# The output projection of a decoder layer: its weight sums made in DRAM, its weight blocks streamed

## The chip, the cores and the metric

The kernel runs on one core of a Trainium2 chip. The metric is the device time of one execution in microseconds (us); lower is better. The time before is the median of three executions.

## The reference

One decoder layer, in float32, for one sequence of 512 tokens and a model width of 2048: adaLN conditioning, one input projection, then two branches (sliding-window attention with sinks, and a gated DeltaNet), a gated merge, and an output projection that is added to the input:

```python
mod = jax.nn.silu(c) @ w_ada + b_ada
shift, scale, gate = jnp.split(mod[:, None, :], 3, axis=-1)
h = rms_norm(x, norm_w) * (1.0 + scale) + shift
proj = h @ w_in
aq, ak, av, ag, d_qkv, dz, db, da, mg_a, mg_b = jnp.split(proj, _split_points(), axis=-1)
...
a_out = swa_attention(aq, ak, av, sinks).astype(x.dtype) * jax.nn.silu(ag)
y_a = a_out @ w_o_swa
...
g = -jnp.exp(a_log.astype(f32)) * jax.nn.softplus(da.astype(f32) + dt_bias.astype(f32))
o = gated_delta_rule(dq, dk, dv, g, beta)
o = rms_norm(o, dn_norm_w) * jax.nn.silu(dz.reshape(B, T, DN_V_HEADS, DN_HEAD_V).astype(f32))
y_b = o.reshape(B, T, DN_VAL).astype(x.dtype) @ w_o_dn

y = jax.nn.sigmoid(mg_a) * y_a + jax.nn.sigmoid(mg_b) * y_b
return x + gate * (y @ w_out)
```

The change concerns the last product, `y @ w_out` (512 × 2048 by 2048 × 2048), and where its weights are prepared.

## The kernel before, in words

**Products.** Every float32 product is made of three products of a reduced type (`mm3`, L237): each operand is split into a high part (`whi`, a cast on ScalarE, L52) and a low part (`wlo`, a subtraction on VectorE, L53), and TensorE makes high × high, high × low and low × high. Weights come in 1 MiB blocks of 128 × 2048 into a pool `wraw` of two buffers (`load_job`, L195, the DMA of L200), and are split by halves of 128 × 1024 into a pool `whl` of three buffers each of `whi` and `wlo`. `channel_tile` (L244) makes one 128-channel output of 48 matmuls from two halves, and calls `pump` after every two triples. `pump` is what interleaves the work: it loads and splits the next weights (`weight_tick`), and takes a step of other generators: `live` ones with delays, `slow` ones with a budget, and `side` ones, which `beside(gen, rate, queue)` registers and which advance by `rate` steps per call.

**Stages.** Startup with the adaLN sums; the keys and decay gates of the DeltaNet, with the triangular solves beside them; the heads of the DeltaNet (16 groups, `heads`); the projection of that branch; attention; and `finish`, which projects the attention's result (`os`, 16 tiles), merges both branches into y (kept in DRAM as `y_d`) and calls `output`.

**The keys' stage around the change.** SP (SyncE) issues almost all DMAs, in the order of its instruction stream. For each head pair the stage issues and computes: `E<-g_rows`, a broadcast row per head; the mask product and `affine_select` on POOL (GpSimd; `decay_mask`, L710); an exponential on ScalarE; a product with the keys' own product on VectorE.

**The output stage.** `output` uses a Strassen-Winograd scheme: seven products m1 to m7 in place of eight, over two column halves n, each product in four pieces: 56 items of 12 matmuls. Their left operands are parts of y: a11, a12 and s3, which the `os` loop keeps, and s1, s2, s4, a22, which the generator `combos` (L1301) makes one step per item from rows of `y_d` (tiles ya and yc; the first eight steps make s1 and s2, the next eight a22 and s4). The right operands are blocks of `w_out` or sums of them: four of the seven products (m7, m5, m6, m4) need a sum. Before the change, three slots a, b, c of two blocks each hold raw blocks (a in `wraw`, b and c in a pool `fraw`), and VectorE adds slots in place (`add`, L1345, the instruction of L1347) ahead of the split, in an order of products m1, m7, m5, m2, m6, m4, m3 that lets each sum be made from the last. Sixteen blocks are loaded. `prep(i)` splits the weights of an item two items ahead; `evict` and `columns` add the products, the gate and the input x and store.

Of the kernel before, what the change touches and what calls it, by code (L numbers as in the profile page):

```python
# [7 lines left out]
F32 = mybir.dt.float32  # L8
# [3 lines left out]
ALU = mybir.AluOpType  # L12
# [4 lines left out]
P = 128  # L17
# [19 lines left out]
class Layer:  # L37
# [552 lines left out]
    def deltanet(self):  # L590
        tc, nc, a = self.tc, self.nc, self.a
        dram = self.dram
        self.lt_d = dram.tile([2, 2, 16, 4, HD, HD], F32, name="lt_d")
        self.lab_d = dram.tile([VH, HD, 4, HD], F32, name="lab_d")
        self.ta_d = dram.tile([2, 16, 4, HD, HD], F32, name="ta_d")
        self.ts_d = dram.tile([2, 2, 16, 4, HD, HD], F32, name="ts_d")
        self.kT_d = dram.tile([KH, P, T], F32, name="kT_d")
        self.k_d = dram.tile([KH, P, T], F32, name="k_d")
        self.o_d = dram.tile([VH, P, T], F32, name="o_d")
        with ExitStack() as ps:  # L600
            self.pmm = ps.enter_context(tc.tile_pool(name="pmm", bufs=2, space=PSUM, reuse_waits="tile"))
            self.ptp = ps.enter_context(tc.tile_pool(name="ptp", bufs=2, space=PSUM, reuse_waits="tile"))
            self.gwk = ps.enter_context(tc.tile_pool(name="gwk", bufs=1, reuse_waits="tile"))
            sol1 = ps.enter_context(tc.tile_pool(name="sol1", bufs=1, side="right", reuse_waits="tile"))
            with ExitStack() as sa:
                wk = sa.enter_context(tc.tile_pool(name="dnA", bufs=2, reuse_waits="tile"))
                sol0 = sa.enter_context(tc.tile_pool(name="sol0", bufs=1, reuse_waits="tile"))
                gp = sa.enter_context(tc.tile_pool(name="gates", bufs=1, reuse_waits="tile"))
                self.go(self.gates(gp), 1)
                self.keys_done, self.solve_in = [], {}  # L610
                self.keep_order = True
                for g in range(NST):
                    self.go(self.keys(wk, g, self.acc_k[g]), 10 + 8 * g)
                for j in range(NFIRST):
                    self.merge_gate("mb", j, self.mb_d)
                self.go(self.solve_load(sol0, 0), 1)
                self.go(self.solve_load(sol1, 1), 1)
                s0 = self.paced(self.solve(sol0, 0, nc.vector), 0.82)
                s1 = self.paced(self.solve(sol1, 1, nc.vector), 0.0)
                for kind, j in self.mixed():  # L620
                    if kind == "k":
                        self.go(self.keys(wk, j, self.channel_tile(f"k{j}")), 0)
                    else:
                        self.merge_gate("mb", j, self.mb_d)
                        if j == KT - 3:
                            s0[1] = 1.2
                for j in range(3):
                    self.merge_gate("ma", j, self.ma_d)
                    if s0 not in self.slow:
                        s1[1] = 1.1  # L630
                self.drain_live()
                self.drain_slow(s0)
                self.keep_order = False
                s1[1] = 0.6
            with ExitStack() as sb:
                wk = sb.enter_context(tc.tile_pool(name="dnB", bufs=2, reuse_waits="tile"))
                self.tt = []
                for n in range(4):
                    t = wk.tile([P, NTB, P], F32, tag=f"tt{n}", name=f"tt{n}", bufs=1)
                    nc.gpsimd.memset(t[HD:P, :, 0:HD], 0.0)  # L640
                    self.tt.append(t)
                for g in range(KH):
                    if g == 8:
                        self.drain_slow(s1)
                    self.heads(wk, g)
                for j in range(3, 5):
                    self.merge_gate("ma", j, self.ma_d)
                self.drain_live()
        self.dump("o", self.o_d)

    def keys(self, wk, g, ps):

# [66 lines left out]
    def solve_load(self, wk, b):  # L719
# [16 lines left out]
        yield 4  # L736
        self.solve_in[b] = A, bet

# [532 lines left out]
    def finish(self):  # L1271
        tc, nc, a = self.tc, self.nc, self.a
        with ExitStack() as es:
            yp = es.enter_context(tc.tile_pool(name="fy", bufs=1, reuse_waits="tile"))
            wk = es.enter_context(tc.tile_pool(name="fwk", bufs=2, reuse_waits="tile"))
            quad = lambda pool, name: tuple(pool.tile([P, 8, 256], F32R, name=name + x) for x in "hl")
            A = {n: quad(yp, n) for n in ("a11", "s3", "a12")}
            lo, hi = slice(0, 256), slice(256, 512)
            with ExitStack() as eo:
                self.pmm = eo.enter_context(tc.tile_pool(name="pmmf", bufs=2, space=PSUM, reuse_waits="tile"))  # L1280
                for j in range(KT):
                    m = wk.tile([P, T], F32, tag="m", name="m")
# [18 lines left out]
    def combos(self, wk, A):  # L1301
# [4 lines left out]
        for second in range(2):  # L1306
            for kt in range(8):
# [15 lines left out]
                n = "s4" if second else "s2"  # L1323
                self.split(A[n][0][:, kt, :], A[n][1][:, kt, :], p[:, lo])

    def output(self, es, wk, A):

        tc, nc, a = self.tc, self.nc, self.a
        pf = es.enter_context(tc.tile_pool(name="pfo", bufs=1, space=PSUM, reuse_waits="tile"))
        fr = es.enter_context(tc.tile_pool(name="fraw", bufs=1, reuse_waits="tile"))  # L1330
        slots = {}

        def load(slot, c, r, nchunk):

            for i in range(2):
                if slot == "a":
                    t = self.wraw.tile([P, 2048], F32, tag="raw", name="raw")
                else:
                    t = fr.tile([P, 2048], F32, tag=f"{slot}{i}", name=f"raw{slot}")
                nc.sync.dma_start(out=t, in_=a["w_out"][2 * c + nchunk, 2 * r + i])  # L1340
                slots[slot, i] = t

        piece = lambda slot, p: slots[slot, p // 2][:, (p % 2) * 1024 : (p % 2) * 1024 + 1024]

        def add(x, y):  # L1345
            def f(p):
                nc.vector.tensor_tensor(out=piece(x, p), in0=piece(x, p), in1=piece(y, p), op=ALU.add)  # L1347

            return f

        order = [
            ("m1", "a11", "a", []),
            ("m7", "s3", "b", [add("a", "b"), add("b", "c")]),
            ("m5", "s1", "a", []),
            ("m2", "a12", "b", []),
            ("m6", "s2", "a", [add("a", "c")]),
            ("m4", "a22", "b", [add("b", "a")]),
            ("m3", "s4", "c", []),
        ]
        items = [(n, m, p) for n in range(2) for m in range(7) for p in range(4)]  # L1360
        ready = {}
        after = {
            ("m1", 3): [], ("m7", 3): [("b", 0, 1)],
            ("m4", 3): [("a", 0, 0), ("b", 1, 0)], ("m3", 3): [("c", 1, 1)],
        }

        def prep(i):
            if i >= len(items):
                return
            n, m, p = items[i]  # L1370
            name, _, slot, sums = order[m]
            for f in sums:
                f(p)
            hi = self.whl.tile([P, 1024], F32R, tag="whi", name="whi")
            lo = self.whl.tile([P, 1024], F32R, tag="wlo", name="wlo")
            self.split(hi, lo, piece(slot, p))
            ready[i] = (hi, lo)
            for s, c, r in after.get((name, p), []):
                if name == "m7":
                    load(s, c, r, n)  # L1380
                elif n == 0:
                    load(s, c, r, 1)

        side = self.combos(wk, A)
        next(side, None)
        load("a", 0, 0, 0)
        load("b", 1, 0, 0)
        load("c", 1, 1, 0)
        todo = []
        keep = {}  # L1390
        ps = {}
# [44 lines left out]
        for i in range(2):  # L1436
            prep(i)
        for i, (n, m, p) in enumerate(items):
            name, s, slot, _ = order[m]
            if p == 0:  # L1440
                for t in range(2):
                    m7 = name == "m7"
                    ps[name, t] = pf.tile([P, T], F32, tag=f"y{t}" if m7 else "r", name=name, bufs=1 if m7 else 6)
            hi, lo = ready.pop(i)
            ah, al = A[s]
            for kk in range(2):
                kt = 2 * p + kk
                w = slice(kk * T, kk * T + T)
                for t in range(2):
                    tsl = slice(t * P, (t + 1) * P)  # L1450
                    self.mm3(ps[name, t], (ah[:, kt, tsl], al[:, kt, tsl]), (hi[:, w], lo[:, w]), kt == 0, kt == 7)
                if kk == 0:
                    prep(i + 2)
                    for f in todo:
                        evict(*f)
                    todo = []
                    next(side, None)
            if p == 3:
                todo.append((n, name))
# [108 lines left out]
```

## Time and profile before

| | |
|---|---|
| runs | 2933.2, 2930.87, 2933.1 us (median 2933.1) |
| span of the profiled execution | 2929.7 us |
| TensorE (PE) busy | 2870.6 us, 98% of the span |
| VectorE (DVE) busy | 1787.2 us, 61% |
| ScalarE (ACT) busy | 1085.1 us, 37% |
| GpSimd (POOL) busy | 243.0 us, 8% |
| bytes moved by DMA | 451.11 MB, 154 GB/s on average |
| output stage (`output`) | about 2752 to 2922 us |

The table is from the profiled execution on the one core, whose span is the time from its first to its last instruction; the runs are timed apart from it. In the rows of the prediction, PE is a matmul, PEld the load of its stationary operand; `x48` counts instructions; "L53" is a line of the kernel before; "<-" names what an operation reads, or what ended a wait. A window's row has its stretch, its length, the busy time of PE, PEld, DVE, ACT and POOL with counts, the clock granted to TensorE (1.00 is full), the busy share of the DMA engines, and GB/s. A row of a group has busy time, the mean of one in ns, and idle time before.

### The profile page before, as it was taken

To read this page: it belongs to the slowest core of one execution; us is meant where nothing else is said; L and a number is where in the kernel's file an instruction comes from. 1 tells how busy PE (TensorE), PEld (TensorE's weight loads), DVE (VectorE), ACT (ScalarE), POOL (GpSimd) and SP (SyncE) were. 2 spreads that over 40 slices of the span, in tenths; PEclk is the share of its full clock that TensorE was granted. 3 is DMA by queue.
4 is the path that set the end of the run, shared out by engine and by line. 5 is a ranking of instruction groups with operands and counts; after the bars stand their busy time and mean duration, and the time that the engine had idled before them with its cause. 6 is when DMAs were issued, how large, how long until landed. Compare 5 with 4: busy or idle time off the path is not lost.

```text
span 2929.7 us, 38073 instructions
## 1 busy us (share of the span) xinstructions
PE 2870.6 (98%) x14556; PEld 2351.2 (80%) x14556; DVE 1787.2 (61%) x2915; ACT 1085.1 (37%) x2113; POOL 243.0 (8%) x204
## 2 busy tenths in 40 slices
PE   8899999999999999999999999999999999999988
PEld 6677888888888888888888788888787877888867
DVE  6775998777776545544444553434655655553697
ACT  4355333333334333333333322212343443432343
POOL 0022211100000110000000000000100000000022
PEclk9999999999999999999999999999999999999999
DMA  9747555633334533333332675554322223375562
GB/s 387 281 147 219 163 169 159 203 109 111 125 113 134 160 116 124 115 122 109 123 109 100 235 263 182 186 172 141 105 89 94 85 89 103 119 262 172 173 194 97
DMA packets 175046, 451.11 MB, mean 154 GB/s; under 512 B 72433, under 2 KB 74993, under 8 KB 138897
## 3 DMA queue, kind: packets, MB, share of 16 engines
q1 hardware_dynamic: 174866, 448.70, 46.1%
q8 instruction: 114, 1.87, 0.3%
q14 instruction: 66, 0.54, 0.1%
HBM read 386.95 MB, written 59.45 MB: 152 GB/s over the span
## 4 chain that ended last, share of the span: by engine, by line
PE 84%; DVE 3%; DMA 2%; issue 1%; ACT 1%; POOL 1%; SPq 0%; POOLq 0%; DVEq 0%; ACTq 0%
PE mm L240 24%; PE mm L242 24%; PE mm L241 24%; DVE wlo L53 1%; PE S L1208 1%; PE pv L918 1%; PE po L937 1%; PE O L1259 1%; PE pP L274 1%; PE po L936 1%; PE pd L933 1%; PE pp L908 1%; PE m L241 1%; PE m L242 1%; PE m L240 1%
## 5 line engine op out<-in xcount | busy, mean ns | idle before, releaser
L240 PE MATMUL mm<-hh,whi 128*128 128x512 f32 x2784 | 1130.7, 406 | 2.3 <-ACT whi L52 1.6
L242 PE MATMUL mm<-hh,wlo 128*128 128x512 f32 x2784 | 1089.6, 391 | 1.3 <-DVE wlo L53 1.3
L241 PE MATMUL mm<-hl,whi 128*128 128x512 f32 x2784 | 1087.3, 391 | 0.0
L53 DVE TENSOR_TENSOR wlo<-raw,whi 128x1024 fp32r<-128x1024 f32 (+1 forms) x452 | 554.4, 1229 | 491.5 <-ACT whi L52 481.7
L52 ACT CAST whi<-raw 128x1024 fp32r<-128x1024 f32 (+1 forms) x452 | 470.7, 1044 | 972.9 <-PE mm L241 927.3
L242 PEld LDWEIGHTS mm<-hh,wlo 128*128 128x128 f32 x2784 | 522.6, 188 | 115.1 <-DVE wlo L53 2.2
L240 PEld LDWEIGHTS mm<-hh,whi 128*128 128x128 f32 x2784 | 523.7, 188 | 112.3 <-issue 8.4
L241 PEld LDWEIGHTS mm<-hl,whi 128*128 128x128 f32 x2784 | 524.2, 188 | 98.7 <-issue 0.4
L240 PE MATMUL mm<-oh,whi 128*128 128x512 f32 x512 | 200.6, 393 | 2.6 <-ACT oh L52 1.7
L242 PE MATMUL mm<-oh,wlo 128*128 128x512 f32 x512 | 199.4, 390 | 0.5 <-DVE wlo L53 0.5
L241 PE MATMUL mm<-ol,whi 128*128 128x512 f32 x512 | 199.5, 390 | 0.1
L865 POOL TENSOR_TENSOR qe<-qe,yq 128x512 f32<-128x512 f32 x32 | 51.4, 1624 | 902.7 <-DMA qe<-eg_rows 836.9
L714 POOL TENSOR_TENSOR E<-E,neg_g 128x512 f32<-128x512 f32 x64 | 78.4, 1224 | 476.2 <-DMA E<-g_rows 342.8
L240 PEld LDWEIGHTS mm<-oh,whi 128*128 128x128 f32 x512 | 96.0, 188 | 24.8 <-ACT oh L52 3.0
L241 PEld LDWEIGHTS mm<-ol,whi 128*128 128x128 f32 x512 | 96.1, 188 | 22.2 <-DVE ol L53 1.3
L764 DVE TENSOR_TENSOR A<-A,atmp 128x62 f32<-128x62 f32 (+30 forms) x124 | 112.9, 911 | 1.5
L242 PEld LDWEIGHTS mm<-oh,wlo 128*128 128x128 f32 x512 | 96.1, 188 | 20.9 <-DVE wlo L53 1.3
L757 DVE TENSOR_TENSOR atmp<-A 128x62 f32<-128x62 f32 (+30 forms) x124 | 109.3, 882 | 1.5
L911 DVE SCALAR_TENSOR_TENSOR r<-pp,neg_eg,vt 128x128 f32<-128x128 f32 x96 | 29.2, 346 | 78.8 <-PE pp L908 77.6
L1232 ACT ACTIVATE sm<-sm,mx,rs 128x256 f32<-128x256 f32 (+1 forms) x128 | 71.7, 561 | 3.3 <-DVE mx L1227 3.3
L580 DVE SCALAR_TENSOR_TENSOR yv<-mm,convh,yv 128x511 f32<-128x511 f32 (+2 forms) x96 | 71.5, 745 | 1.6
L241 PE MATMUL m<-wlo,hh 128*128 128x512 f32 x128 | 51.8, 404 | 10.1 <-DVE wlo L53 10.1
(331 smaller groups left out, 3145.6 us busy)
## 6 DMA issues: line engine op xcount, KB each, us to landing
raw<-in_w_ch SPq DMA_DIRECT2D x158, 1024.0 KB
wa<-in_w_ada_ss SPq DMA_DIRECT2D x32, 1024.0 KB
raw<-in_w_od SPq DMA_DIRECT2D x32, 1024.0 KB
E<-g_rows SPq DMA_DIRECT2D x64, 256.0 KB
gw<-in_w_ada_gate SPq DMA_DIRECT2D x16, 1024.0 KB
raw<-in_w_os SPq DMA_DIRECT2D x16, 1024.0 KB
qe<-eg_rows SPq DMA_DIRECT2D x32, 256.0 KB
o_d<-zh SPq DMA_DIRECT2D x32, 256.0 KB
```

Of the source, the lines that this page charges most:

```text
L52: self.nc.scalar.copy(out=hi, in_=src)
L53: self.nc.vector.tensor_tensor(out=lo, in0=src, in1=hi.bitcast(F32), op=ALU.subtract)
L240: nc.tensor.matmul(ps, lhsT=wh, rhs=xh, start=first, stop=False)
L241: nc.tensor.matmul(ps, lhsT=wh, rhs=xl, start=False, stop=False)
L242: self.last_mm = nc.tensor.matmul(ps, lhsT=wl, rhs=xh, start=False, stop=last).ins
L274: self.nc.tensor.transpose(dst[:, c * P : (c + 1) * P], src_cols(c), self.ident)
L580: nc.vector.scalar_tensor_tensor(out=y[:, s:], in0=ps[:, : T - s], scalar=w[:, j : j + 1], in1=y[:, s:], op0=ALU.mult, op1=ALU.add)
L714: nc.gpsimd.tensor_tensor(out=E, in0=E, in1=ng, op=ALU.add)
L757: eng.tensor_tensor(out=t, in0=A[:, m : m + 1, m + 1 :].to_broadcast([P, m, n]), in1=A[:, :m, m : m + 1].to_broadcast([P, m, n]), op=ALU.mult,
L764: eng.tensor_tensor(out=A[:, :m, m + 1 :], in0=A[:, :m, m + 1 :], in1=t, op=ALU.add)
L865: nc.gpsimd.tensor_tensor(out=qf, in0=qf, in1=q, op=ALU.mult)
L1232: nc.scalar.activation(t, t, AF.Exp, scale=r[:, h : h + 1], bias=mx[:, h : h + 1], accum_out=den[:, h : h + 1])
```

## The change

The four sums for each of the four block positions (two column halves n, two row halves i) are made in DRAM, into sixteen new tensors `ws_d` of 1 MiB, by the DMA engines: a block or an earlier sum is copied within DRAM on SP, then a second block is added to it by an accumulating transfer that POOL issues. m7 and m5 are each a copy and an accumulate of blocks; m6 copies m7 and adds a block; m4 copies m6 and adds another. `weight_sums` is registered with `beside` at the start of the heads' stage, at a rate of 0.15 steps per call.

The output stage then loads 28 blocks, one for each two items, in the order of their use: blocks of `w_out` for m1, m2, m3 and the sums for the rest, into a pool of four buffers (`out_load`). The first four are loaded ahead of the `os` loop, each next one when a block's second piece has been split. The additions on VectorE are gone. The order of the products becomes m1, m2, m7, m5, m6, m4, m3: m2 moves ahead of m7 and m5.

```diff
+        self.ws_d = {k: dram.tile([P, 2048], F32, name=f"ws{k[0]}{k[1]}{k[2]}") for k in self.sum_keys()}
...
+                self.beside(self.weight_sums(), 0.15, "ws")
                 for g in range(KH):
...
                 self.drain_live()
+                self.drain("ws")
...
+    def weight_sums(self):
+        nc = self.nc
+        for n in range(2):
+            for i in range(2):
+                w = lambda c, r: self.a["w_out"][2 * c + n, 2 * r + i]
+                m7, m5, m6, m4 = (self.ws_d[s, n, i] for s in ("m7", "m5", "m6", "m4"))
+                steps = [
+                    [(m7, w(1, 0), w(1, 1)), (m5, w(0, 0), w(1, 0))],
+                    [(m6, m7, w(0, 0))],
+                    [(m4, m6, w(0, 1))],
+                ]
+                for parts in steps:
+                    for dst, src, _ in parts:
+                        nc.sync.dma_start(out=dst, in_=src)
+                    for _ in range(2):
+                        yield
+                    for dst, _, more in parts:
+                        nc.gpsimd.dma_start(out=dst, in_=more, accum_op=ALU.add, max_dma_last_dim=8192)
+                    for _ in range(2):
+                        yield
...
+            self.wpool = es.enter_context(tc.tile_pool(name="fraw", bufs=4, reuse_waits="tile"))
+            for _ in range(4):
+                self.out_load()
...
+    def out_order(self):
+        return [
+            ("m1", "a11", (0, 0)), ("m2", "a12", (0, 1)), ("m7", "s3", None), ("m5", "s1", None), ("m6", "s2", None),
+            ("m4", "a22", None), ("m3", "s4", (1, 1)),
+        ]
+
+    def out_load(self):
+        j = self.wnext
+        if j < 28:
+            n, m, i = j // 14, j // 2 % 7, j % 2
+            name, _, q = self.out_order()[m]
+            t = self.wpool.tile([P, 2048], F32, tag="raw", name="raww")
+            src = self.a["w_out"][2 * q[0] + n, 2 * q[1] + i] if q else self.ws_d[name, n, i]
+            self.nc.sync.dma_start(out=t, in_=src)
+            self.wtiles[j] = t
+            self.wnext += 1
...
-        def add(x, y):
-            def f(p):
-                nc.vector.tensor_tensor(out=piece(x, p), in0=piece(x, p), in1=piece(y, p), op=ALU.add)
...
-            name, _, slot, sums = order[m]
-            for f in sums:
-                f(p)
             hi = self.whl.tile([P, 1024], F32R, tag="whi", name="whi")
             lo = self.whl.tile([P, 1024], F32R, tag="wlo", name="wlo")
-            self.split(hi, lo, piece(slot, p))
+            self.split(hi, lo, self.wtiles[i // 2][:, (i % 2) * 1024 : (i % 2) * 1024 + 1024])
             ready[i] = (hi, lo)
-            for s, c, r in after.get((name, p), []):
-                if name == "m7":
-                    load(s, c, r, n)
-                elif n == 0:
-                    load(s, c, r, 1)
+            if i % 2:
+                del self.wtiles[i // 2]
+                self.out_load()
```

A scheduler orders each engine's instructions, so where the new ones stand does not follow from the code alone. SP (SyncE), at the end of the startup and the first head pair of the keys' stage, before:

```order
L354 DMA wa<-in_w_ada_ss 128x2048 x2
L200 DMA raw<-in_w_ch 128x2048 x3
L495 DMA v_d<-vt 128x512 x2
L506 DMA sums<-in_k_sums 128x512
L508 DMA al<-in_a_log 128x32
L510 DMA dtb<-in_dt_bias 128x32
L200 DMA raw<-in_w_ch 128x2048
L266 DMA mb_d<-mth 128x512
L568 DMA g_rows<-rows 32x512
```

The same place after the change. The names wsm_1141, 1145, 1149, 1153 are the sums m7, m5, m6, m4 of the first block position, wsm_1142 is m7 of the second:

```order
L671 DMA wsm_1141<-in_w_out 16x16384
L200 DMA raw<-in_w_ch 128x2048
L495 DMA v_d<-vt 128x512 x2
L671 DMA wsm_1145<-in_w_out 16x16384
L506 DMA sums<-in_k_sums 128x512
L508 DMA al<-in_a_log 128x32
L510 DMA dtb<-in_dt_bias 128x32
L671 DMA wsm_1149<-wsm_1141 16x16384
L200 DMA raw<-in_w_ch 128x2048
L671 DMA wsm_1142<-in_w_out 16x16384
L266 DMA mb_d<-mth 128x512
L671 DMA wsm_1153<-wsm_1149 16x16384
```

The copies stand here, among the weight loads of the keys' stage, and not with the heads; `g_rows` follows the last row. A copy that reads an earlier sum (wsm_1149, wsm_1153) follows the accumulate that completes it, which is on POOL. Ten of the sixteen copies stand between here and the third head pair's rows, the other six some seventy rows later in the same stage.

POOL (GpSimd), from the first mask product of the keys' stage on, before:

```order
L714 ISA
L714 TENSOR_TENSOR E<-E,neg_g 128x512
L715 AFFINE_SELECT E<-E 128x512
L714 TENSOR_TENSOR E<-E,neg_g 128x512
L715 AFFINE_SELECT E<-E 128x512
```

After, with the accumulates under the names of the sums that they complete:

```order
L675 DMA wsm_1141<-in_w_out 128x2048
L675 DMA wsm_1145<-in_w_out 128x2048
L675 DMA wsm_1149<-in_w_out 128x2048
L675 DMA wsm_1142<-in_w_out 128x2048
L675 DMA wsm_1153<-in_w_out 128x2048
L675 DMA wsm_1146<-in_w_out 128x2048
L742 ISA
L742 TENSOR_TENSOR E<-E,neg_g 128x512 x2
L743 AFFINE_SELECT E<-E 128x512 x2
L675 DMA wsm_1150<-in_w_out 128x2048
```

Six accumulates now stand ahead of the first mask product, and the others between later ones. VectorE, in the output stage, before (ya, yc are the operands of `combos`, hl, hh its splits, raw and rawb the weight slots):

```order
L1347 TENSOR_TENSOR raw<-raw,rawb 128x1024
L53 TENSOR_TENSOR a12l<-m,a12h 128x256
L1313 TENSOR_TENSOR ya<-ya,yc 128x256
L1347 TENSOR_TENSOR rawb<-rawb,rawc 128x1024
L53 TENSOR_TENSOR wlo<-raw,whi 128x1024
L1319 TENSOR_SCALAR ya<-ya 128x256
L53 TENSOR_TENSOR hl<-ya,hh 128x256
L1347 TENSOR_TENSOR raw<-raw,rawb 128x1024
```

After, at the same place of the stage:

```order
L1345 TENSOR_TENSOR ya<-ya,yc 128x256
L1351 TENSOR_SCALAR ya<-ya 128x256
L53 TENSOR_TENSOR wlo<-raww,whi 128x1024
L53 TENSOR_TENSOR hl<-ya,hh 128x256 x2
L53 TENSOR_TENSOR wlo<-raww,whi 128x1024
L1345 TENSOR_TENSOR ya<-ya,yc 128x256
L1351 TENSOR_SCALAR ya<-ya 128x256
```

The additions of L1347 are gone, and the splits of weights (wlo) stand closer together between the same steps of `combos`.

More of the change, by code (lines that the diff above doesn't have):

```diff
@@ L648, in deltanet, with sum_keys @@
                 self.drain_live()
+                self.drain("ws")
         self.dump("o", self.o_d)
+    def sum_keys(self):
+        return [(s, n, i) for s in ("m7", "m5", "m6", "m4") for n in range(2) for i in range(2)]
+    def weight_sums(self):
[18 more added lines that the diff above has]
+                        yield
     def keys(self, wk, g, ps):
@@ L1277, in finish @@
             A = {n: quad(yp, n) for n in ("a11", "s3", "a12")}
+            self.wtiles, self.wnext = {}, 0
+            self.wpool = es.enter_context(tc.tile_pool(name="fraw", bufs=4, reuse_waits="tile"))
+            for _ in range(4):
+                self.out_load()
             lo, hi = slice(0, 256), slice(256, 512)
@@ L1329, in output @@
         pf = es.enter_context(tc.tile_pool(name="pfo", bufs=1, space=PSUM, reuse_waits="tile"))
[L1330 to L1343, printed above, removed]
-        def add(x, y):
-            def f(p):
[L1347 to L1359, printed above, removed]
+        order = self.out_order()
         items = [(n, m, p) for n in range(2) for m in range(7) for p in range(4)]
         ready = {}
[L1362 to L1365, printed above, removed]
         def prep(i):
@@ L1369, in prep @@
                 return
-            n, m, p = items[i]
-            name, _, slot, sums = order[m]
-            for f in sums:
-                f(p)
             hi = self.whl.tile([P, 1024], F32R, tag="whi", name="whi")
             lo = self.whl.tile([P, 1024], F32R, tag="wlo", name="wlo")
-            self.split(hi, lo, piece(slot, p))
+            self.split(hi, lo, self.wtiles[i // 2][:, (i % 2) * 1024 : (i % 2) * 1024 + 1024])
             ready[i] = (hi, lo)
-            for s, c, r in after.get((name, p), []):
-                if name == "m7":
-                    load(s, c, r, n)
-                elif n == 0:
-                    load(s, c, r, 1)
+            if i % 2:
+                del self.wtiles[i // 2]
+                self.out_load()
         side = self.combos(wk, A)
         next(side, None)
-        load("a", 0, 0, 0)
-        load("b", 1, 0, 0)
-        load("c", 1, 1, 0)
         todo = []
@@ L1438, in output @@
         for i, (n, m, p) in enumerate(items):
-            name, s, slot, _ = order[m]
+            name, s, _ = order[m]
             if p == 0:
```

## The prediction

> **What bounds the kernel now.** I read the page first, then the windows of the two stages that the change touches, then single engines in them.
>
> ```profile
> PE 2870.6 (98%) x14556; PEld 2351.2 (80%) x14556; DVE 1787.2 (61%) x2915; ACT 1085.1 (37%) x2113; POOL 243.0 (8%) x204
> L53 DVE TENSOR_TENSOR wlo<-raw,whi 128x1024 fp32r<-128x1024 f32 (+1 forms) x452 | 554.4, 1229 | 491.5 <-ACT whi L52 481.7
> ```
>
> TensorE is busy 98% of the span, so a microsecond can be won only where it pauses or crawls, and is lost wherever a new wait starves it. The windows say where. Their columns are the stretch, its length, busy time of PE, PEld, DVE, ACT and POOL, the granted clock, the DMA share and GB/s.
>
> ```profile
> 127.00:217.00 90.00, 84.51 (x396) 67.49 (x397) 60.80 (x125) 44.65 (x107) 14.64 (x15) 0.98 0.48 152
> 217.00:317.00 100.00, 94.67 (x460) 76.76 (x459) 62.71 (x128) 45.67 (x111) 23.75 (x26) 1.00 0.67 200
> 317.00:420.00 103.00, 103.00 (x482) 85.52 (x481) 95.82 (x133) 40.08 (x89) 21.04 (x15) 1.00 0.54 166
> 2752.00:2922.00 170.00, 158.11 (x674) 127.38 (x673) 155.21 (x197) 71.47 (x93) 33.96 (x14) 0.97 0.49 158
> 2752.00:2812.00 60.00, 56.56 (x244) 44.90 (x243) 56.46 (x98) 33.28 (x54) 0.00 (x0) 1.00 0.56 172
> 2810.00:2830.00 20.00, 14.05 (x49) 10.82 (x48) 19.29 (x25) 6.37 (x9) 4.50 (x3) 0.74 0.76 251
> ```
>
> From 2752 on (the output products) VectorE is busy 155.2 of 170 us, far above its 61% of the span, and TensorE is not full: 158.1. In the slice at 2810 VectorE has 19.3 of 20 us and TensorE 14.1, at a clock of 0.74. TensorE's own rows, and its waits from 2730 on (total, times, longest):
>
> ```profile
> 2752.27 0.39 PE L240 MATMUL m<-whi,a11h 128*128 128x512 f32 x1
> 2763.15 0.39 PE L240 MATMUL m<-whi,s3h 128*128 128x512 f32 x1
> ...
> 2816.94 0.80 PE L241 MATMUL m<-wlo,hh 128*128 128x512 f32 x1 [5.95 <-DVE wlo L53]
> 2817.54 0.63 PE L242 MATMUL m<-whi,hl 128*128 128x512 f32 x1
> 2817.97 0.63 PE L241 MATMUL m<-wlo,hh 128*128 128x512 f32 x1
> ...
> 2921.43 0.39 PE L242 MATMUL m<-whi,hl 128*128 128x512 f32 x1
> PE m L241 <- DVE wlo L53: 11.6, 6, 5.9
> ```
>
> The first product's 48 matmuls take 2763.15 − 2752.27 = 10.88 us, 0.227 each. The stage has 7 products × 2 column halves × 4 pieces × 12 = 672 matmuls: 152.3 us if dense. It lasts to 2921.8, 169.5, so 17.2 us are lost. Of these 11.6 are waits for VectorE's low halves. Behind the longest, rows stand 0.43 us apart instead of 0.227 (2817.54 to 2817.97): some 14 matmuls at the low clock, 14 × 0.2 = 2.8 us. The remainder is small gaps.
>
> **The change part by part.**
>
> *Sums off VectorE.* These rows go; the streamed blocks are split as they are:
>
> ```profile
> L1347 DVE TENSOR_TENSOR rawb<-rawb,raw 128x1024 f32<-128x1024 f32 x8 | 10.8, 1356 | 0.1
> L1347 DVE TENSOR_TENSOR raw<-raw,rawc 128x1024 f32<-128x1024 f32 x8 | 9.8, 1223 | 0.1
> L1347 DVE TENSOR_TENSOR raw<-raw,rawb 128x1024 f32<-128x1024 f32 x8 | 9.7, 1219 | 0.0
> L1347 DVE TENSOR_TENSOR rawb<-rawb,rawc 128x1024 f32<-128x1024 f32 x8 | 9.7, 1219 | 0.0
> ```
>
> 32 adds, 40.0 us. VectorE's stage falls from 155.2 to 115 of 170 us. With 56 items, an item then costs it 115/56 = 2.1 us against 12 × 0.227 = 2.7 on TensorE: TensorE leads again. The upper end of the gain is the whole 17.2 us.
>
> *m2 ahead of m7, sums s1, s2, s4 as before.* The first eight steps of the combinations, one per item, make s1 and s2. Their first user, m5, was the third product and is now the fourth: four items, 10.9 us, later. No cost; what it wins is in the 17.2.
>
> *28 blocks instead of 16.* Twelve MiB more, 12.6 MB. The nearest rate is a stretch with the DMA full:
>
> ```profile
> 100.00:120.00 20.00, 18.35 (x134) 13.58 (x132) 16.80 (x22) 5.00 (x8) 0.00 (x0) 1.00 0.99 386
> ```
>
> At 386 GB/s that is 32.6 us, while the stage's share of 0.49 leaves 170 × 0.51 = 87 idle: room on the whole. It is tight early. A block lasts two items, 5.44 us, or 193 GB/s. The operand rows of the combinations, in the same queue, come on top: 2752 to 2812 moved 172 GB/s altogether, of which the weights were a part. Together I estimate 310 to 380 of 386 GB/s for the first 44 us, so some operand arrives late and with it a split. Four blocks in hand cover 22 us of this. I keep back 4 of the 17.2: gain 13, ends 8 (half of the waits stay as DMA waits) and 17.
>
> *The sums in DRAM, and where they run.* They are put beside the heads, but stand far ahead in the queues: ten of the sixteen copies on SP between the last weight loads of the startup and the third head pair's, that is from the first of these rows on (about 127 to 230 us), and six around the last two (some 330 to 380 us).
>
> ```profile
> 127.33 10.68 SPq L200 DMA_DIRECT2D raw<-in_w_ch  x2
> 140.87 0.50 SPq L510 DMA_DIRECT2D dtb<-in_dt_bias  x1
> 150.76 0.33 SPq L200 DMA_DIRECT2D raw<-in_w_ch  x1
> 158.87 0.34 SPq L568 DMA_DIRECT2D g_rows<-rows  x1
> 163.85 0.35 SPq L200 DMA_DIRECT2D raw<-in_w_ch  x1
> ...
> 337.37 0.33 SPq L200 DMA_DIRECT2D raw<-in_w_ch  x1
> 371.56 0.54 SPq L200 DMA_DIRECT2D raw<-in_w_ch  x1
> ```
>
> No row of before is a copy within DRAM or an accumulating transfer. Bounds: a copy of 1 MiB takes 2.7 us at 386 GB/s if each byte counts once, 5.4 if reading and writing count apart. An accumulate takes 2.7 to 8.2 (it also reads its target). I take 2.7 + 5.4 = 8.1 a pair, nearest to the weight loads' row, which have one DRAM end: 16 × 8.1 = 130 us. The idle DMA time of 127 to 420 is 90 × 0.52 + 100 × 0.33 + 103 × 0.46 = 127 us. So the pairs just fit, and what they cost is order: SP and POOL run in turn, and a copy that reads an earlier sum waits for that accumulate with everything on SP behind it (weight loads, g_rows, E); each accumulate on POOL waits for its copy, with the mask products of E behind it.
>
> Step by step, at 8.1 a pair: the first copy goes at 127.7 and lands by 133 to 134, its accumulate by 141. The copy that waits for it is issued behind the `dtb` row at 141.4, so SP loses nothing. The copy for the fourth block waits for that accumulate in turn, until about 157 to 160, with g_rows (158.9) behind it: 0 to 3 us. The load at 163.85 may then slip by as much. Weight loads bear this: whl holds three halves, wraw two blocks, and a late load of 5 us is covered by five halves × 5.44 less splitting and landing, some 17 us. The masks bear less:
>
> ```profile
> 173.58 1.05 POOL L714 TENSOR_TENSOR E<-E,neg_g 128x512 f32<-128x512 f32 x1 [173.14 <-DMA E<-g_rows]
> 177.30 0.65 POOL L715 TENSOR_SCALAR_AFFINE_SELECT E<-E 128x512 f32<-128x512 f32 x1
> 183.46 1.14 ACT L684 ACTIVATE E<-E 128x512 f32<-128x512 f32 x2
> ```
>
> POOL starts the first pair's masks at 173.58 and ends them at 177.95; ScalarE takes them up at 183.46: 5.5 us to spare. Six accumulates now stand ahead of the first row on POOL. Cost taken: 4 us of TensorE, ends 0 and whatever the rival below makes.
>
> One rule of the Trainium skill speaks against this part: "DMA: Bandwidth & Descriptors", section "Latency and other measured facts", has copies within DRAM at 207 to 214 GB/s in each direction. By it a copy would be an estimated 5 us and a pair at my accumulate 10.4, not 8.1, so the result would be that of the first rival; no row here shows it.
>
> *The sum*, against the profiled execution: 2929.7 − 13 + 4 = 2920.7 span. The median of the runs lies 3.4 above that span (2933.1): 2924 us.
>
> **The rivals.**
>
> 1. *Slower: the early sums block SP and POOL.* If a pair takes more than (127 idle + 17 slack + 13 gain)/16 = 9.8 us, the front loses more than the output wins. For it: the DMA of 217 to 317 is already at 0.67, and chains of four transfers follow each other (copy, accumulate, copy, accumulate), each step with a landing of some 2.7 us beyond its bytes, as the last small transfer shows:
>
> ```profile
> 2918.83 3.39 DMA x<-in_x
> ```
>
> (256 KB, 0.7 us of bytes at 386 GB/s.) At 10.8 a pair: 173 − 127 − 17 = 29 us lost, 2933.1 − 13 + 29 = 2949. At the upper bounds, 13.6 a pair, 218 − 144 = 74 lost: 2994. Against it: 10 of 16 pairs are the early ones, and accumulates that are merely late hurt nobody but the next copy.
>
> 2. *Same: VectorE's wait becomes a DMA wait.* Operands and blocks share the queue; if every late split stays late for its operand's sake, only the waits from the second half (2810 on) go: some 8 us of wait and slow clock gained, 4 lost in front: 2929, within 0.2% of 2933.1 (5.9 us, about what a measurement of this kernel can tell from no change). For it, the 0.76 of DMA share in the slice at 2810; against it, four blocks in hand.
>
> 3. *The sums do not run where the change says.* Sure in part, since they stand by the keys' stage and not the heads'. Were they executed late after all, with the heads, whose DMA has more room, the front would cost nothing: 2920.
>
> **How the numbers follow.** Forecast 0.38, third rival 0.05, together the 0.43 of faster; second rival, same, 0.17; first rival, slower, 0.40, since nothing in the trace prices an accumulating transfer, and the pair that decides (9.8) is close to my 8.1. The likeliest time is 2924, its own range 2914 (17 gained, 1 to 2 lost) to 2930. To hold eight in ten the range must take in most of the slower case: up to 2965, where a pair would take 11.8 us (189 − 144 = 45 lost, 2933.1 − 13 + 45).
>
> **What would show it.** Right: in the output stage VectorE near 115 us, TensorE's 672 matmuls in 153 to 161 us at a clock of 1.00, no L1347 adds; copies and accumulates as transfers of 8 us a pair between 127 and 380 us; TensorE there with at most 4 us of new waits. Wrong in the first rival's way: SP standing at a copy for an accumulate, waits of VectorE or ACT for raw or E between 140 and 400 us, a lower clock there, and the output reached late by tens of microseconds. Wrong in the second's: waits on the combinations' operands or on raww in place of the 11.6 us. A pair outside 5.4 to 13.6 us would refute the price; an output stage still over 165 us would refute the main gain.

## The result, and the profile after

The changed kernel takes 2981.3 us (median of 5 runs, 2980.0 to 2985.0), the kernel before 2933.1: a ratio of 1.0166, 95% interval 1.0154 to 1.0179. It is 48 us slower, where 9 us faster was forecast, and lies above the stated range (2914 to 2965). The first rival had the sign and the place, though not the price.

Where the time went shows in one operation that both kernels have: the first product of the heads' stage on TensorE. The view of the tile `py`, of before and then of after (durations in ns, then first and last start in us):

```profile
L877 PE MATMUL py<-ta,lab x256: 218/218/267, 562.5 to 1575.0; 64*64 64x64 f32 x128
```

```profile
L905 PE MATMUL py<-ta,lab x256: 218/218/267, 618.1 to 1631.1; 64*64 64x64 f32 x128
```

It starts 55.6 us later, and the last one 56.1 us later: the whole loss is made ahead of the heads' stage, and nothing is added in it. The rest of the account is in the output stage. TensorE's rows after, at the first and the last matmul of the output stage and at its longest gap:

```profile
2807.88 0.39 PE L240 MATMUL m<-whi,a11h 128*128 128x512 f32 x1
...
2878.63 0.79 PE L240 MATMUL m<-whi,hh 128*128 128x512 f32 x1 [2.37 <-ACT hh L52]
...
2972.25 0.39 PE L242 MATMUL m<-whi,hl 128*128 128x512 f32 x1
```

The stage starts 55.6 us late and ends 50.8 late (2972.25 − 2921.43): it won 4.8 us, not 13. So −4.8 + 55.6 = +50.8 us in the profiled executions (spans 2929.7 and 2980.0). The stage's window, and TensorE's waits for low halves in it, which were 11.6 us:

```profile
2807.00:2973.00 166.00, 157.82 (x677) 126.76 (x675) 120.99 (x167) 71.52 (x93) 25.52 (x14) 0.99 0.72 250
```

```profile
PE m L241 <- DVE wlo L53: 5.0, 5, 1.8
```

VectorE is no longer full (121 of 166 us, before 155 of 170).

The windows of the keys' stage after (columns as before):

```profile
127.00:217.00 90.00, 77.12 (x336) 61.22 (x336) 41.59 (x79) 32.32 (x70) 9.98 (x12) 0.92 0.92 274
217.00:317.00 100.00, 78.98 (x355) 64.16 (x356) 51.02 (x124) 46.18 (x121) 26.75 (x32) 0.86 0.79 229
317.00:420.00 103.00, 98.52 (x451) 80.74 (x451) 77.71 (x124) 37.06 (x75) 18.80 (x21) 0.98 0.83 252
```

The DMA share rose from 0.48, 0.67, 0.54 to 0.92, 0.79, 0.83. In the first 90 us TensorE made 336 matmuls instead of 396; the granted clock was 0.92 there and 0.86 in the next 100 us, before 0.98 and 1.00. That clock is a second price. From 127 to 472 us the trace's record of it shows 0.5, for 3.4 to 10.2 us each time, at nine of TensorE's ten gaps of 2.3 us or more, and the matmuls of the projections (`mm`) then start 0.43 us or more apart instead of 0.23.

### The profile page after: what moved, and what is told of

It is laid out like the page before. It is cut to its first block, busy times and chain, and to the rows that moved or that the text cites. A ratio compares the mean times of both kernels' runs of the same rounds, so it can differ in the third digit from the quotient of the medians.

```text
span 2980.0 us, 38116 instructions
## 1 busy us (share of the span) xinstructions
PE 2887.5 (97%) x14556; PEld 2362.6 (79%) x14556; DVE 1743.3 (59%) x2883; ACT 1087.4 (36%) x2113; POOL 240.3 (8%) x220
## 5 line engine op out<-in xcount | busy, mean ns | idle before, releaser
L53 DVE TENSOR_TENSOR wlo<-raw,whi 128x1024 fp32r<-128x1024 f32 (+1 forms) x428 | 523.8, 1227 | 522.6 <-ACT whi L52 518.3
L52 ACT CAST whi<-raw 128x1024 fp32r<-128x1024 f32 (+1 forms) x428 | 445.1, 1043 | 940.7 <-PE mm L241 904.0
L53 DVE TENSOR_TENSOR wlo<-raww,whi 128x1024 fp32r<-128x1024 f32 x56 | 70.8, 1268 | 26.2 <-ACT whi L52 24.7
L52 ACT CAST whi<-raww 128x1024 fp32r<-128x1024 f32 x56 | 58.8, 1052 | 59.7 <-PE m L242 46.1
## 6 DMA issues: line engine op xcount, KB each, us to landing
wsm<-in_w_out POOLq DMA_DIRECT2D x16, 1024.0 KB, 12.4
```

The source lines that it names most:

```text
L52: self.nc.scalar.copy(out=hi, in_=src)
L53: self.nc.vector.tensor_tensor(out=lo, in0=src, in1=hi.bitcast(F32), op=ALU.subtract)
```

## What the waits look like

TensorE's waits from 127 to 472 us of the changed kernel (total, times, longest):

```profile
PE ptkT L274 <- ACT k L696: 13.4, 2, 8.9
PE mm L240 <- ACT whi L52: 9.2, 3, 6.3
PE ptk L274 <- DVE y L587: 7.7, 4, 2.9
PE ptk L274 <- DVE rkt L63: 7.6, 1, 7.6
PE pg L543 <- DVE gy L536: 4.0, 1, 4.0
```

The nine rows of this view add to 48.9 us. Before, in the same window, they add to 11.2, the longest being:

```profile
PE v L240 <- ACT hh L433: 3.8, 2, 3.3
PE ptkT L274 <- ACT k L668: 3.5, 3, 1.7
```

So some 38 of the 55.6 us are waits; the other 18 are, by subtraction, what the slow matmuls add. No single cause stands there: the five rows shown are waits for VectorE or ScalarE. One step behind the longest of them stand transfers that land late, for `mm` the weight loads (1 MiB), for the others smaller ones (16 to 256 KB). The gates are the first case. SP's issue of `dtb` (16 KB) after, and VectorE's use of it, before and then after, with a later row of VectorE after:

```profile
140.90 0.46 SPq L510 DMA_DIRECT2D dtb<-in_dt_bias  x1
```

```profile
146.52 0.23 DVE L522 TENSOR_TENSOR gy<-bd,dtb 128x128 f32<-128x128 f32 x1
154.90 0.29 DVE L522 TENSOR_TENSOR gy<-bd,dtb 128x128 f32<-128x128 f32 x1 [4.12 <-DMA dtb<-in_dt_bias]
181.59 0.68 DVE L567 COPY rows<-pr 32x512 f32<-32x512 f32 x1 [11.53 <-DMA g_rows<-rows]
```

Before, the issue stands at 140.87, and VectorE uses it 5.6 us later without a wait. Now 16 KB take 14.0 us from issue to use, with the same queue ahead of them on SP but for two copies of 1 MiB. The last row is VectorE's wait of 11.5 us for the write of g_rows (64 KB). The rows that go into g_rows, the copy (m4) that stands ahead of it on SP, and its issue:

```profile
164.79 0.68 DVE L567 COPY rows<-pr 32x512 f32<-32x512 f32 x1 [1.21 <-PE pr L565]
173.68 0.48 SPq L671 DMA_DIRECT2D wsm<-wsm  x1
174.25 0.53 SPq L568 DMA_DIRECT2D g_rows<-rows  x1
```

The masks follow from that: POOL's first `affine_select` starts at 197.1 us, before at 174.7.

ScalarE's waits for masks and for weight loads in the same stretch, and POOL's rows ahead of ScalarE's two longest waits for masks (8.6 us until 218.6, and 7.9 us until 265.2, just behind POOL's mask, though the trace puts it down to lt_d):

```profile
ACT E L712 <- POOL E L743: 30.3, 9, 8.6
ACT whi L52 <- DMA raw<-in_w_ch: 16.7, 4, 11.0
216.14 1.04 POOL L742 TENSOR_TENSOR E<-E,neg_g 128x512 f32<-128x512 f32 x1 [16.37 <-DMA E<-g_rows]
263.36 1.05 POOL L742 TENSOR_TENSOR E<-E,neg_g 128x512 f32<-128x512 f32 x1 [7.72 <-DMA E<-g_rows]
```

At both, POOL itself waits for a row of E to land, and not for one of the copies. The weight loads, which the prediction took to be covered, hold ScalarE for 16.7 us, where before it has no such wait; the longest ends just ahead of TensorE's wait of 6.3 us at 448 us.

The accumulates themselves, in the view of their line (total and number of POOL's waits ahead of them, of which 134.6 us are the idle time from the start of the kernel to the first):

```profile
L675 POOL DMA_DIRECT2D wsm<-in_w_out x16: 802/816/990, 135.1 to 432.7; - x16
...
  DMA wsm<-in_w_out: 194.8, 6
  DMA wsm<-wsm: 72.4, 8
...
DMA to landing us min/median/max: 8.7/12.4/16.0
```

The queue that carries them has its own row on the page:

```profile
q0 software_dynamic: 2304, 16.78, 2.9%
```

2.9% of 16 engines' 2980 us is 86 us of all engines, 5.4 us an accumulate. The copies' packets (64 KiB each) add to 40.3 us, 2.5 a copy. A pair costs 7.9 us of DMA time, against a forecast of 8.1.

## The experiments

Lag means how much later the first product of the heads' stage starts than in the kernel before (562.5 us). It can shift by 1 to 3 us between executions: kernels without sums in front show −0.9 to 2.2.

**The front alone, and the output alone.**

```diff
 (e1: the kernel before, with weight_sums registered as in the change; nothing reads ws_d)
 (e2: the changed kernel without weight_sums)
-            src = self.a["w_out"][2*q[0]+n, 2*q[1]+i] if q else self.ws_d[name, n, i]
+            q = q or {"m7": (1, 0), "m5": (0, 0), "m6": (1, 1), "m4": (0, 1)}[name]
+            src = self.a["w_out"][2*q[0]+n, 2*q[1]+i]
```

> The sums are made in DRAM at the same places of the queues as in the changed kernel, but nobody reads them: the output stage is that of the kernel before, with its additions on VectorE. Theory (the early sums cost the keys' stage 56 us, read from the matmuls of equal number, which run 55.6 us later in the changed kernel from matmul 2200 on): 2933 + 56 = 2989 us, 2.0% slower, the whole lag gained by matmul 2200. Rival (part of the lag comes from the rest of the change, for example other orders on PE or VectorE): under 2970 us.

> The streamed output stage of the changed kernel with no sums made: the blocks of m7, m5, m6 and m4 are read from unsummed blocks of w_out, so the sums are left out of the result. Theory (the streamed stage wins the 5 us by which the lag falls in it, 55.6 to 50.8 us): 2928 us, 0.17% faster, the last 672 matmuls in 164 to 165 us, 5 us of waits for low halves and 2 to 3 for the operands of the combinations. Rival (the 13 us of the prediction are there, and the sums in DRAM or the late start took them): 2920 us, the 672 matmuls in 157 us.

Measured: e1 2987.0 us, ratio 1.0189 (1.0175 to 1.0203), lag 52.3. e2 2927.7 us, ratio 0.9984 (0.9975 to 0.9992), 672 matmuls in 165.5 us, before 169.2. The two parts are independent and nearly add up. The streamed stage is worth 5 us, so the 13 us were not hidden by the sums or the late start, and the sums cost 54.

**Another place.**

```diff
-                        for dst, src, _ in parts:
-                            nc.sync.dma_start(out=dst, in_=src)
+                        with self.behind():
+                            for dst, src, _ in parts:
+                                nc.sync.dma_start(out=dst, in_=src)
 (e3; the accumulates likewise. e7: so held, and registered at the start of attention)
```

> Each copy and each accumulate is held behind the last matmul issued when it is registered, so that SP and POOL reach it in the heads' stage, where the change says it runs. Theory (the loss is the place, not the transfers): the matmuls up to number 2200 as before, within 2 us; heads' stage at most 5 us longer, since its DMA share is 0.3 to 0.4; 2928 to 2933 us. Rival (the transfers cost wherever they run, as chains that SP and POOL wait for): the lag of some 50 us appears between matmuls 4000 and 8000 instead, 2970 us or more.

> As the run held to the heads, but the sums are registered at the start of attention, where the DMA share is 0.2 to 0.3. Theory: no stage longer than before by over 1 us, the output stage's 4 to 5 us won: 2928 to 2929 us, 0.15% faster. Rival (the transfers hold up attention's own small transfers and POOL's rope products): a lag of 5 us or more there, 2933 us or more.

e3: 2933.3 us, ratio 1.0006 (0.9997 to 1.0015). The keys' stage is as before (lag −0.9). One wait is new in the heads, at their first product:

```profile
PE py L907 <- DMA lab<-lab_d: 3.8, 1, 3.8
```

With the slow matmuls behind it, `py` takes 7 us longer from first to last than before, more than the 5 expected, and the output stage still starts 5.4 us late: this takes what the output gains. The DMA share from 560 to 1060 us is 0.63, before 0.40. e7: 2927.1 us, ratio 0.9982 (0.9973 to 0.9991). Attention takes no longer, at a DMA share of 0.51 to 0.54 (before 0.28 to 0.29), though POOL stands longer for the copies there, 192 us against 133 behind the first accumulate of the changed kernel. The waits of e7 from 2050 to 2600 us:

```profile
POOL wsm L675 <- DMA wsm<-wsm: 173.8, 7, 46.4
POOL wsm L675 <- DMA wsm<-in_w_out: 17.8, 2, 14.8
```

The same transfers, then, cost 54 us, 6 us or nothing by where they stand.

**Order or bytes.** In the keys' stage two things could cause the loss: engines that stand in order behind transfers, or the load of the transfers.

```diff
 (e4: no copy waits for an accumulate)
-                    [(m6, m7, w(0, 0))],
-                    [(m4, m6, w(0, 1))],
+                    [(m6, w(1, 0), w(0, 0))],
+                    [(m4, w(0, 0), w(0, 1))],
 (e5: output as in e2, and)
-                        nc.sync.dma_start(out=dst, in_=src)
+                        nc.sync.dma_start(out=dst[:, :128], in_=src[:, :128])
 (e5, the accumulates: likewise dst[:, :128] and more[:, :128])
 (e6: no accumulates; e9: accum_op=ALU.add left out; e10: accumulates of [:, :1024])
 (e11: held as in e3, registered at the keys' first tile, 0.3 steps per call)
```

> As the changed kernel, but m6 and m4 start from copies of w_out blocks and not from earlier sums (part of their sums is left out): the same number and size of transfers at nearly the same places, without a copy on SP that waits for an accumulate. Theory A (SP standing at such copies, with weight loads and mask rows behind it, makes most of the loss): 2981 - 35 = 2946 us or less. Theory B (POOL standing at accumulates, or the DMA load of 7.9 us a pair, makes it): 2970 us or more.

> The 16 copies and 16 accumulates of the changed kernel with all their waits, on the first 128 of 2048 columns only; the output stage reads unsummed blocks of w_out, so most of the sums is left out of the result. All 32 stand early on SP and POOL, all 16 accumulates ahead of the first mask product: the order and the standing are there, the bytes are not (a sixteenth). Theory (the bytes make the loss: with the DMA engines at 0.8 to 0.9 busy, the small transfers of the keys' stage land late): a lag of at most 12 us by matmul 2400, and 2928 + 12 = 2940 us or less. Rival (engines that stand in order behind copies and accumulates make it): a lag of 30 us or more, 2960 us or more.

> The changed kernel without its accumulates, at the same places on SP; the sums in the result are left out. What remains is 16 copies of 2.5 us of DMA time (40 us in place of 126) and copies that wait for copies on SP. Theory (bytes): the DMA has room for 40 us, a lag of 5 to 20 us, 2935 to 2950 us. Rival (SP standing, which remains): a lag of 35 us or more.

> The changed kernel with each accumulate replaced by a plain copy of the same block by POOL; both queues' order and every wait are the same, instruction for instruction, the sums are left out of the result. DMA time falls from 7.9 to an estimated 5.1 us a pair (two copies of 2.5), and a copy that waits for such a transfer waits less long. Theory (the accumulate's own slowness, 5.3 us of DMA time and 12 us to landing, makes the loss): a lag of at most 15 us by matmul 2400, 2945 us or less. Rival (32 transfers of 1 MiB that wait for each other in order make it, whatever they do): a lag of 30 us or more, 2958 us or more.

> The changed kernel with accumulates of 1024 of the 2048 columns, at nearly the same places; half of the sums is left out of the result. Some 43 us of accumulates in place of 85. If the lag comes from the sum of DMA time over the idle time: it falls by far more than half, to under 15 us (2945 us or less). If it goes in proportion to the accumulates: 25 to 30 us (2953 to 2958 us). If it is set by order and not by bytes: over 45 us.

> All sums in the keys' stage, as in the changed kernel, but held behind matmuls and spread evenly from 150 to some 400 us, each accumulate two steps (about 10 us) behind its copy, so that POOL and SP seldom stand for one. Theory A (the DMA's load in this stage is the cause): a lag of 35 us or more, 2963 us or more. Theory B (the standing and the bunching are the cause: ten pairs in the first 100 us): a lag of 15 us or less, 2943 us or less.

| run | DMA time of the sums, us | lag, us | time, us | ratio (95% interval) |
|---|---|---|---|---|
| e5 tiny sums | 9 (accumulates) | 3.1 | 2932.4 | 0.9998 (0.9989 to 1.0007) |
| e6 copies only | 43 | 3.1 | 2932.4 | 1.0002 (0.9992 to 1.0011) |
| e9 plain in place | 89 | 23.8 | 2949.7 | 1.0063 (1.0043 to 1.0082) |
| e10 half accumulates | 98 | 28.1 | 2955.0 | 1.0078 (1.0063 to 1.0093) |
| e11 spread in keys | 130 | 32.9 | 2961.0 | 1.0095 (1.0080 to 1.0110) |
| e4 no chain | 124 | 51.7 | 2978.2 | 1.0159 (1.0145 to 1.0173) |
| as changed | 125 | 55.6 | 2981.3 | 1.0166 (1.0154 to 1.0179) |

(The DMA time is the sum of the packets' times in the trace, over 16 engines.) e5 has all 32 transfers and their waits, closer together and all ahead of the first mask, and loses next to nothing: order alone isn't it. e6 loses less than the 5 us expected at least. e4 takes away SP's waits for accumulates, and its lag of 51.7 us is that of e1 (52.3), which has them: no gain that can be told. Its first g_rows shows why. SP sends it at 164.2 us instead of 174.25, but it lands 16 us later instead of 7, and VectorE goes on at 180.3 instead of 181.6. e9 has the order of the changed kernel, instruction for instruction; only what the second transfer does differs (its issue on POOL also takes 0.53 us instead of 0.82), and over half of the lag goes. POOL stands almost as long for the copies in it (118 us behind the first, in the changed kernel 133), so it isn't shorter standing that saved that half. Its theory gave at most 15 us of lag and its rival at least 30, and 23.8 were found: the accumulate's slowness is the larger part and not the whole. Its view of the accumulates' line, against 12.4 us after:

```profile
DMA to landing us min/median/max: 5.8/9.6/12.0
```

Among the kernels with the change's early order the lag climbs with DMA time: 3 at 43 us, 24 at 89, 28 at 98, 52 to 56 at 125. e10 thus fell out as the line in proportion said, and not under 15 us as a threshold at the idle time would have it. e11 met neither theory (35 or more, 15 or less): spread evenly, the full load costs 33, not 56. The remaining 23 may be the bunching (ten pairs in the first 130 us). In e11 the losses go with the load too, as its windows show, though POOL also stands 81 us for copies in it:

```profile
127.00:217.00 90.00, 81.58 (x376) 64.64 (x375) 57.95 (x105) 42.33 (x100) 14.23 (x14) 0.97 0.62 190
217.00:317.00 100.00, 90.18 (x422) 72.73 (x421) 49.00 (x119) 43.68 (x112) 25.69 (x29) 0.96 0.86 251
317.00:420.00 103.00, 91.12 (x399) 74.97 (x400) 84.21 (x122) 34.68 (x68) 18.65 (x18) 0.92 0.98 294
```

Where the share is 0.62, TensorE keeps 376 of 396 matmuls; at 0.98 it falls to 399 where before made 482. The share alone doesn't set the loss: from 420 to 472 us of e11 it is 1.00, and TensorE makes 239 matmuls, before 244. The early kernels and e11 differ in place as well as in spread, so this split is rough. Not tried: the load without any standing (the same bytes in independent transfers at the same time).

**Where the output's other 8 us were.** The groups of the output stage of the changed kernel show operands that arrive late (busy, mean ns, idle before and its cause):

```profile
L52 ACT CAST hh<-yc 128x256 fp32r<-128x256 f32 x8 | 3.3, 407 | 14.6 <-DMA yc<-y_d 14.6
L1345 DVE TENSOR_TENSOR ya<-ya,yc 128x256 f32<-128x256 f32 x16 | 6.8, 423 | 10.1 <-DMA ya<-y_d 6.5 <-DMA yc<-y_d 3.4
```

These tiles share two buffers with the products c11, u2, c22 and two with x, and TensorE's longest gap (2878.63 above) waits for `hh`, a split of them.

```diff
-                p = wk.tile([P, T], F32, tag="m", name="ya")
+                p = wk.tile([P, T], F32, tag="ya", name="ya", bufs=3)
-                q = wk.tile([P, T], F32, tag="yb", name="yc")
+                q = wk.tile([P, T], F32, tag="yc", name="yc", bufs=3)
 (e8, on e7; fraw gets bufs=2, and every second pair of blocks goes to wraw)
 (e12: the kernel before, bufs=3 for the tag "yb")
```

> As the run before, and the operands of the combinations get buffers of their own, three each, in place of two that they share with the products and with x; the streamed blocks use two buffers of their own pool and the two of wraw, so that two blocks and not four are in hand ahead of the os loop. Theory (the rest of the loss in the output stage is operands that come late because SP stands for their shared buffers): the 672 matmuls in 156 to 159 us, 2921 to 2924 us. Rival (they are late by the DMA's load of 0.8, or the later blocks are): 163 to 166 us, 2928 us or more.

> The kernel before, with its additions on VectorE, and a third buffer (the only one that fits) for the tiles yb, yc and x that share a name. Theory (before the change VectorE's additions, not the operands, set the output stage): 2931 to 2935 us, the 672 matmuls in 168 to 170 us. Rival (the buffers alone give the gain of the run with own buffers): 2926 us or less, the stage in 163 us or less.

e8: 2918.3 us, ratio 0.9958 (0.9944 to 0.9971): 12 us faster than before, the fastest of all. TensorE's rows at the first and last matmul of its output stage, and the window:

```profile
2750.93 0.39 PE L240 MATMUL m<-whi,a11h 128*128 128x512 f32 x1
...
2906.58 0.39 PE L242 MATMUL m<-whi,hl 128*128 128x512 f32 x1
```

```profile
2750.00:2907.00 157.00, 154.81 (x677) 126.23 (x675) 118.20 (x152) 68.19 (x85) 25.92 (x14) 1.00 0.72 246
```

155.7 us for 672 matmuls, 152.3 being dense: 13.5 won over before, at a DMA share of 0.72, the same as in the changed kernel's stage. TensorE's waits in the stage fall from 7.7 us in the changed kernel to 2.0. So the load alone did not make the operands late there; with buffers of their own they came in time. Stage and time are a little better than was expected. (e8 has also two blocks in hand instead of four ahead of the `os` loop; the two were not separated.) e12: 2930.1 us, ratio 0.9994 (0.9985 to 1.0003), no difference that can be told, though its profiled stage was 165.9 us, which lies between the two expectations. One buffer is less than e8's, so it shows only that this smaller step isn't enough by itself.

## Why the prediction was wrong, point by point

- *Output stage, 13 us won (ends 8 and 17)*: 4.8 found, below the lower end. VectorE came to 121 us (115 forecast). The blocks in hand did their part: no engine waits for `raww` in the stage. The term that failed is the 4 us kept back for late operands: 12.4 of the 17.2 were lost. That is the second rival's mechanism, at a cause it didn't name: e8 points to the shared buffers and not to the queue's bytes. With buffers of their own the term measures 13.5.
- *A pair at 8.1 us*: 7.9 measured (copies 2.5, accumulates 5.4). The price was right; that the accumulate's 5.4 was met so closely is luck, since it was picked between 2.7 and 8.2 with no row to go by. The Trainium skill ("DMA: Bandwidth & Descriptors", section "Latency and other measured facts") gives 207 and 214 GB/s for copies of 16 KiB rows between HBM tensors, in each direction, at a row pitch of 512 KiB and at a padded pitch of 4 MiB; by them a copy would take an estimated 5 us. For the contiguous blocks here the trace shows 2.5 us of DMA time. So a dearer copy is not what made the change slower, and the first rival, which needed 9.8 us a pair, had the sign by a price that wasn't there.
- *"So the pairs just fit, and what they cost is order", 4 us*: this is the step that made the forecast wrong: 55.6. The 127 idle microseconds were added up over 293 us and treated as free. The runs show in its place that the bytes cost, and long before the idle time is used up: nothing clear at 43 us of added DMA time, 24 us of lag at 89. The stage's chain runs over transfers (dtb, g_rows, E, late weight loads too) that land later, some 38 us of waits, and TensorE's clock then adds some 18. A threshold of 9.8 us a pair decides nothing: at 7.9 the loss was already there, and with halved accumulates (6.1 a pair) half of it. Nor did "weight loads bear this" with its 17 us of slack hold: they held ScalarE for 16.7 us.
- *First rival, SP and POOL blocked*: right in sign and place. Of its mechanism, SP's waits for accumulates are in the trace, but e4 without them has the lag of e1, and e5 shows that the order without the bytes costs next to nothing. POOL's standing behind full-size copies, with the masks behind it, is in every run with a large lag. e9 and the two longest waits for masks speak against it as the main cause, but no run has the load without any standing.
- *The chain of the sums on SP, 0 to 3 us for g_rows*: g_rows went out at 174.25 instead of 158.87, 15.4 us late. Its rows were ready at 165.5 instead of 158.8, 6.6 us late, because of the gates (dtb). The other 8.8 are SP, which stood 12.9 us at the copy ahead of g_rows for the accumulate of m6, where the prediction had this copy at 157 to 160. So this term was mis-sized as well, but with the stand taken away (e4) VectorE goes on only 1.3 us earlier.
- *Third rival*: the early place was certain from the order, and the time as if in the heads (2920) wasn't met even there: e3 2933, since the heads cost 6 us by the start of the output stage and the output gave 4.

## What to carry to other kernels

Idle DMA time in a stage isn't room for large transfers if the stage's own critical chain runs over transfers: cost them by how late a 16 KB transfer lands there, and try bulk work in the stages one after the other (in attention it cost 0 us here, against 54; why attention bears it was not tested, its DMA share before is 0.29 and that of the keys' stage 0.48 to 0.67). Read from the order where a scheduler has put work "beside" another stage, and pin it. And a stage that is freed of one engine's work shows its next limit at once, here two shared operand buffers, worth some 9 us from e7 to e8: look for it in the waits of the second engine before counting the gain.

## What the runs showed of the hardware

An accumulating transfer within DRAM moved 8 KiB packets in 0.63 us, where plain ones of that size take 0.31 in the same trace (median of the packets): twice the DMA time, 5.4 us against 2.5 a MiB. A copy within DRAM took no more DMA time than a weight load into SBUF: 2.43 us for a packet of 64 KiB, where eight packets of 8 KiB take 2.47. And a 16 KB load took 14.0 us from issue to use while copies of 1 MiB and an accumulate were under way, and at most 5.6 before the change.
